# Decoder layer on one core: 512 weight columns where tokens stand, the first loads in turn, other loads and splits moved in the front

## The chip, the cores and the metric

The kernel runs on one core of one Trainium2 chip. The metric is the time of one execution on the device in microseconds (us). Five engines work beside each other, each in the order of its own program: TensorE (PE, matmuls and transposes), VectorE (DVE), ScalarE (ACT), GpSimd (POOL) and SyncE (SP, which only issues DMAs here). They wait for each other by semaphores.

## The reference

256 tokens of 1024 features pass one decoder layer in float32: a token mixer, cross attention into 256 memory tokens, and a top-4-of-32 mixture of experts, each followed by a layer norm with a residual.

```
proj = x @ w_in      # 1024 x 3600: ml q,k,v,o, gates i,f, gd q,k,v,z, gates b,a
h_ml = rms_norm(mlstm_chunkwise(q, k, v, i_pre, f_pre)) * sigmoid(ml_o)
qkv  = silu(causal_depthwise_conv([gd_q, gd_k, gd_v], gd_conv))
h_gd = rms_norm(gated_delta_chunkwise(l2(q), l2(k), v, g, beta)) * silu(gd_z)
x    = layer_norm(alpha * x + concat(h_ml, h_gd) @ w_out)
x    = layer_norm(alpha * x + softmax((x wq)(mem wk)^T / 16) (mem wv) @ wo)
x    = layer_norm(alpha * x + sum over the 4 best experts of gate * swiglu(x w_gu) w_down)
```

The weights of the first two parts have some 31 MB, those of the experts 403 MB.

## The kernel before

The program has a front (mixer and cross attention) and the expert stage behind it. In the front the weights come through a ring of six buffers of 1 MB, most as 1024 rows x 256 columns, loaded on SP's queue in the order of use (class Block, L193). `split` (L216) cuts a half of a block (128 x 1024 elements on the chip) into two fp32r parts that sum to it: the upper part is a copy on ACT (L225), the lower a subtraction (L226) on DVE, or on POOL for the second halves of the blocks named in `pool_split` (L235). The parts lie in three buffers named `whl`. `products` (L237) then makes three matmuls for each pair of tiles: upper by upper (L275), lower by upper and upper by lower (L277, L278). In some products features stand (weights are the stationary operand and 256 tokens stream); in others tokens stand and 256 weight columns stream: mv, mo, gz (parts of w_in), wout, wv and wxo.

ORDER (L36) gives the order of the w_in blocks: gk, gv, gq, gz are key, value, query and gate z of the gated delta heads, mk, mv, mq, mo those of the mLSTM heads. Between the products run "lanes" (class Lanes, L54): generators that issue a few instructions, tell for how long the engine PE is kept busy and after how long they want to go on, and wait for names that others put into a set. The lanes that matter here:

- `gates` (L397): the product of x with the gate columns (ps_g), tanh on ACT (r_f, r_i, RA; L415 to L417), softplus by exp and ln (r_e, r_t), scans on DVE (cum L434, RD L438). Then PE transposes RA and RD (ps_c, L449, L450).
- `post_k` (L490): convolution and silu of the keys (kT, L488, on DVE), then the transposes of the keys on PE (ps_t, L500), once the gates are done. `post_v` has the same for the values (vy, L488; ps_t, L521).
- `gdn_prepare` (L560) forms the matrices of the delta rule (ps_gb, ps_kk, dl, du, ps_nt), `solve` (L655) solves them, `mlstm_pair` has sd from ps_cm (L838 to L845).
- `post_res` (L929) adds the residual (L933) and takes the statistics (L934) of the layer norm.

gk0's load and x's (transposed) load are in quarters, x first. The broadcast loads of four norm vectors are issued on ACT's queue at the start.

Of the kernel before, what the change touches and what calls it, by code (L numbers as in the profile page):

```python
# [35 lines left out]
ORDER = "gk0 mv0 gk1 mk0 mq0 gq0 gv0 mo0 mv1 gv1 gz0 gq1 mo1 gz1"  # L36
# [74 lines left out]
def kernel(  # L111
# [62 lines left out]
    xt_in = chunk("xt_in").rearrange("p (k t) -> p k t", k=KT)  # L174
    for q in range(4):
        nc.sync.dma_start(xt_in[:, 2 * q:2 * q + 2, :], x_t[q * 256:q * 256 + 256, :].rearrange("(k p) t -> p k t", p=P))
# [13 lines left out]
    gph, gpl = (wt([P, 2, KT, 4, 32], "whl", F32R, n, bufs=3)[:, 0] for n in ("gph", "gpl"))  # L190
# [4 lines left out]
    class Block:  # L195


        def __init__(self, src, c0, name, then=None, rows=None):
            self.src, self.c0, self.name, self.then, self.rows = src, c0, name, then, rows

        def load(self):
            if self.rows is not None:
# [3 lines left out]
                self.parts = [None, None]  # L206
                return
            self.tv = chunk(self.name).rearrange("p (k c) -> p k c", k=KT)
            for ks in [slice(k, k + 2) for k in (0, 2, 4, 6)] if self.name == "gk0" else (slice(0, KT),):
                nc.sync.dma_start(self.tv[:, ks, :],  # L210
                                  self.src[0, ks.start * P:ks.stop * P, self.c0:self.c0 + 256].rearrange("(k p) c -> p k c", p=P))
            if self.then is not None:
                self.then()
            self.parts = [None, None]

        def split(self, hf):  # L216

            if self.parts[hf] is not None:
                return
            both = wt([P, 2, 4, 256], "whl", F32R, bufs=3)  # L220
            hi, lo = both[:, 0], both[:, 1]
            eng = nc.gpsimd if self.name in pool_split and hf == 1 else nc.vector
            for ks in (slice(0, 2), slice(2, 4)) if self.name == "gk0" else (slice(0, 4),):
                src = self.tv[:, hf * 4:hf * 4 + 4][:, ks] if self.rows is None else self.tv[:, :, hf * 256:hf * 256 + 256]
                i = nc.scalar.activation(hi[:, ks], src, AF.Copy)  # L225
                j = eng.tensor_sub(lo[:, ks], src, hi[:, ks])  # L226
                if self.name == "gk0":
                    pin(i)
                    pin(j)
            self.parts[hf] = (hi, lo)  # L230
            done.add((self.name, hf))

    pool_split = ("gk1", "mk0", "gv0", "mq0", "gv1", "gq0", "gq1", "wk0", "wk1")

    def products(pieces):  # L235


        blocks = []
        for p in pieces:
            if p["blk"] not in blocks:  # L240
                blocks.append(p["blk"])
        loaded, cut, banks = [0], [0], {}

        def ahead(i):
            n = blocks.index(pieces[min(i, len(pieces) - 1)]["blk"])
# [3 lines left out]
            while cut[0] < len(pieces) and cut[0] <= i + (2 if i else 1):  # L249
                pieces[cut[0]]["blk"].split(pieces[cut[0]]["part"])  # L250
                cut[0] += 1

        for n, p in enumerate(pieces):
            blk, hf, fresh = p["blk"], p["hf"], False
            if p["ready"] is not None and not p["ready"]():
                ahead(n - 1)
                yield p["ready"]
            ahead(n)
# [5 lines left out]
            for j in p["js"]:  # L264
                o = ps[:, j * T:j * T + T]
                js = slice(j * P, j * P + P)
                for k4 in range(4):
                    k = hf * 4 + k4
                    kx = k if blk.rows is None else k4
                    if p["feat"]:  # L270
                        a = (wh[:, k4, js], wl[:, k4, js], xh[:, kx, :], xl[:, kx, :])
                    else:
                        a = (xh[:, kx, js], xl[:, kx, js], wh[:, k4, :], wl[:, k4, :])

                    nc.tensor.matmul(o, a[0], a[2], start=fresh, stop=False, skip_group_check=True)  # L275
                    fresh = False
                    nc.tensor.matmul(o, a[0], a[3], start=False, stop=False, skip_group_check=True)  # L277
                    nc.tensor.matmul(o, a[1], a[2], start=False, stop=(k == KT - 1), skip_group_check=True)  # L278
                    if p["fine"]:
                        yield 0.32  # L280
                if not p["fine"]:
                    yield 1.28
            for lane in p["after"]:
                lanes.add(lane(ps), 0.3)
# [104 lines left out]
    for q in range(4):  # L389
# [3 lines left out]
        if q == 0:  # L393
            pin(nc.scalar.activation(gph[:, :, :, 0:4], gst, AF.Copy))
            pin(nc.vector.tensor_sub(gpl[:, :, :, 0:4], gst, gph[:, :, :, 0:4]))

    def gates():  # L397
# [9 lines left out]
        yield 2.6, 0.3  # L407
# [82 lines left out]
    def post_k(hp):  # L490
        def lane(ps):
# [5 lines left out]
            yield from wait("gates")  # L497
# [63 lines left out]
    def gdn_prepare():  # L561
# [55 lines left out]
        for c in range(2):  # L617
            lanes.add(solve(c), 1.5 * c)
        rsqrt(rk, ssq, rkt)
# [1121 lines left out]
```

## Time and profile before

| | us |
|---|---|
| median of 3 runs | 1254.56 |
| lowest, highest | 1253.55, 1255.59 |
| the profiled execution | 1253.94 |
| its span in the profile | 1252.3 |
| first expert matmul in it | 304.35 |

In that execution PE has work for 1162.0 us (93% of the span), DVE for 395.4, ACT for 242.4 and POOL for 76.7. In the second part of the page the span stands in 40 slices of 31.3 us. The first ten are the front: there DVE is busy at 5 to 8 tenths, and the DMA engines at 2 to 9. In the others PE and DMA stand at 9, and the DMA engines move 416 to 418 GB/s.

### The profile page before, as it was taken

How to read it: one execution, taken by the hardware profiler on the slowest of the kernel's cores; microseconds unless marked ns; L12 is line 12 of the kernel's file. 1: busy time of each engine (PE TensorE's matmuls, PEld its weight loads, DVE VectorE, ACT ScalarE, POOL GpSimd, SP SyncE). 2: the span in 40 equal slices, each digit the busy share in tenths (PEclk: the TensorE clock that was granted, in tenths of full speed). 3: DMA queues.
4: the chain of work that ended last, by engine and by line, in shares of the span. 5: the costliest groups of instructions: out<-in, count | busy, mean ns of one | idle time of the engine just before them, and what ended most of it. 6: DMA issues, size and time to landing. Idle time of an engine off the chain costs nothing. (4 is left out here: it accounts for less than half of the span.)

```text
span 1252.3 us, 15908 instructions
## 1 busy us (share of the span) xinstructions
PE 1162.0 (93%) x6521; PEld 618.0 (49%) x6521; DVE 395.4 (32%) x967; ACT 242.4 (19%) x448; POOL 76.7 (6%) x91
## 2 busy tenths in 40 slices
PE   7899999999999999999999999989999799999895
PEld 7889899997434343443434332323233334323244
DVE  7786888565211111121111111111121112111124
ACT  5445544452101110101111010101010001100011
POOL 5241130003000000000000000000000000000001
PEclk9899999999999999999999999999999899999998
DMA  9523268787999999999999999999999999999996
GB/s 326 184 75 102 69 209 313 269 322 282 395 374 418 416 417 417 417 418 417 417 418 417 416 417 417 416 417 417 417 416 417 417 405 418 416 417 418 417 353 167
DMA packets 125176, 446.67 MB, mean 357 GB/s; under 512 B 8550, under 2 KB 57958, under 8 KB 92330
## 3 DMA queue, kind: packets, MB, share of 16 engines
q1 hardware_dynamic: 124092, 443.63, 89.8%
q10 hardware_dynamic: 1008, 1.99, 0.4%
q8 instruction: 53, 0.87, 0.3%
q14 instruction: 23, 0.19, 0.0%
HBM read 444.54 MB, written 1.05 MB: 356 GB/s over the span
## 5 line engine op out<-in xcount | busy, mean ns | idle before, releaser
L107 PE MATMUL ps_glu<-gu,xe 128*64 128x512 f32 x1024 | 268.5, 603 | 22.5 <-DMA gu<-in_exp_w_gu_dram 16.1
L107 PE MATMUL ps_lin<-gu,xe 128*64 128x512 f32 x1024 | 264.2, 594 | 0.0
L107 PE MATMUL ps_y<-dn,ay 128*64 128x512 f32 (+1 forms) x1216 | 233.5, 530 | 19.8 <-DMA dn<-in_exp_w_down_dram 12.1
L1461 DVE TENSOR_SCALAR glu<-ps_glu 128x512 f32<-128x512 f32 x30 | 20.8, 692 | 534.6 <-PE ps_glu L107 534.6
L107 PEld LDWEIGHTS ps_y<-dn,ay 128*64 128x64 f32 x1216 | 78.7, 136 | 157.1 <-issue 113.0
L107 PEld LDWEIGHTS ps_glu<-gu,xe 128*64 128x64 f32 x1024 | 67.7, 137 | 175.3 <-issue 115.5
L107 PEld LDWEIGHTS ps_lin<-gu,xe 128*64 128x64 f32 x1024 | 74.1, 138 | 147.4 <-issue 147.1
L1462 ACT ACTIVATE glu<-glu 128x512 f32<-128x512 f32 x30 | 18.9, 630 | 514.8 <-DVE glu L1461 514.8
L1496 DVE COPY ay<-ps_y 64x512 f32<-64x512 f32 x29 | 20.0, 689 | 170.2 <-PE ps_y L107 170.2
L107 PE MATMUL acc<-ay,gp 128*128 128x512 f32 (+1 forms) x152 | 61.6, 547 | 3.7 <-DVE ay L1496 2.9
L107 POOL TENSOR_TENSOR o<-o,gb 128x512 f32<-128x512 f32 x3 | 4.2, 1409 | 936.6 <-DVE rs L107 934.4
L107 PE MATMUL ps_x<-oh,x 128*128 128x128 f32 x512 | 60.3, 275 | 1.3 <-DVE oh L1282 1.1
L107 PEld LDWEIGHTS ps_x<-oh,x 128*128 128x128 f32 x512 | 59.6, 192 | 3.6 <-DVE oh L1282 1.3
L1473 ACT ACTIVATE ay<-ps_at 128x512 f32<-128x512 f32 x30 | 17.9, 597 | 115.8 <-PE ps_at L107 115.8
L107 PEld LDWEIGHTS acc<-ay,gp 128*128 128x128 f32 x152 | 24.3, 189 | 32.2 <-issue 15.0
L1425 DVE TENSOR_SCALAR ohg<-iom,rank,Gh 128x64 f32<-128x64 f32 x120 | 33.2, 309 | 11.9 <-PE ps_x L107 11.9
L1441 ACT ACTIVATE bs<-ident 128x256 fp32r<-128x256 f32 x30 | 12.2, 411 | 99.7 <-PE ps_gp L107 94.1
L107 PE MATMUL ps_at<-ident,glu 128*128 128x128 f32 x128 | 20.9, 286 | 11.2 <-DVE gp L1429 11.2
L107 PEld LDWEIGHTS ps_at<-ident,glu 128*128 128x128 f32 x128 | 13.5, 140 | 27.8 <-DVE gp L1429 14.8
L1351 ACT ACTIVATE xe<-ps_x 128x512 f32<-128x512 f32 x32 | 19.1, 597 | 36.0 <-PE ps_x L107 36.0
L1465 DVE SCALAR_TENSOR_TENSOR glu<-glu 128x512 f32<-128x512 f32 x30 | 20.6, 688 | 0.0
L1464 DVE SCALAR_TENSOR_TENSOR glu<-glu 128x512 f32<-128x512 f32 x30 | 20.6, 685 | 0.0
(505 smaller groups left out, 1688.1 us busy)
## 6 DMA issues: line engine op xcount, KB each, us to landing
gu<-in_exp_w_gu_dram SPq DMA_DIRECT2D x256, 1024.0 KB, 19.9
dn<-in_exp_w_down_dram SPq DMA_DIRECT2D x120, 1024.0 KB, 20.0
dn<-in_exp_w_down_dram SPq DMA_DIRECT2D x14, 512.0 KB, 7.4
wout<-in_w_out_dram SPq DMA_DIRECT2D x4, 1024.0 KB, 4.9
wk<-in_xa_wk_dram SPq DMA_DIRECT2D x4, 1024.0 KB, 7.1
wv<-in_xa_wv_dram SPq DMA_DIRECT2D x4, 1024.0 KB, 6.4
wq<-in_xa_wq_dram SPq DMA_DIRECT2D x4, 1024.0 KB, 5.0
wxo<-in_xa_wo_dram SPq DMA_DIRECT2D x4, 1024.0 KB, 5.0
```

Of the source, the lines that this page charges most:

```text
L107: return lambda *a, **k: self.tc.keep_in_program_order(f(*a, **k))
L1351: nc.scalar.activation(xe_of(b)[:, q * 4:q * 4 + 4, :], ps.rearrange("p (k s) -> p k s", k=4), AF.Copy)
L1425: nc.vector.tensor_scalar(og_[:, c, j], iom, rk[c][j], gh[c][j], ALU.is_equal, ALU.mult)
L1441: nc.scalar.activation(bs.rearrange("p (q s) -> p q s", q=4), sel.unsqueeze(2).to_broadcast([P, 4, 64]), AF.Copy)
L1461: nc.vector.tensor_scalar(gl, pgu[0], 7.0, None, ALU.min)
L1462: nc.scalar.activation(th, gl, AF.Tanh, scale=0.851)
L1464: nc.vector.scalar_tensor_tensor(li, li, 1.0, gl, ALU.add, ALU.mult)
L1465: nc.vector.scalar_tensor_tensor(li, th, 1.0, li, ALU.add, ALU.mult)
L1473: nc.scalar.activation(act[1][:, b], pv, AF.Copy)
L1496: nc.vector.tensor_copy(act[2][rows_of(b, 0), 0, :], py[rows_of(b, 0), :])
```

## The change

1. **512 columns.** The weights of mv, mo, gz, wout, wv and wxo are loaded as 512 rows x 512 columns, and one matmul streams 512 columns where two streamed 256. A split now covers 256 rows x 512 columns, and the work that follows such a product goes by halves of the tokens.
2. **Start.** The quarters of x and gk0 are loaded in turn, gk0's products stand between the products of the gates, and gk0's parts have two of the three `whl` buffers, the gates' weights the third.
3. **Loads.** The four broadcast loads go from ACT's queue at the start to SP's queue behind gq0.
4. **Splits.** gv0, gv1, gq1 leave `pool_split`, and the lower part of mem (L1024) goes from POOL to DVE.
5. **Keys.** Their transposes wait for `rk` (the end of gdn_prepare) in place of `gates`. The first two solve lanes get a delay of 3.0 before the rsqrt.
6. **Order.** "gk0 mv gk1 mk0 mq0 gq0 gv0 mo gv1 gq1 gz", and the second mLSTM pair waits for the first.

```diff
-ORDER = "gk0 mv0 gk1 mk0 mq0 gq0 gv0 mo0 mv1 gv1 gz0 gq1 mo1 gz1"
+ORDER = "gk0 mv gk1 mk0 mq0 gq0 gv0 mo gv1 gq1 gz"
...
     for q in range(4):
-        nc.sync.dma_start(xt_in[:, 2 * q:2 * q + 2, :], x_t[q * 256:q * 256 + 256, :].rearrange("(k p) t -> p k t", p=P))
+        qs, rows = slice(2 * q, 2 * q + 2), slice(q * 256, q * 256 + 256)
+        nc.sync.dma_start(xt_in[:, qs, :], x_t[rows, :].rearrange("(k p) t -> p k t", p=P))
+        nc.sync.dma_start(gk0_in[:, qs, :], w_in[0, rows, C_GK:C_GK + 256].rearrange("(k p) c -> p k c", p=P))
...
-    gph, gpl = (wt([P, 2, KT, 4, 32], "whl", F32R, n, bufs=3)[:, 0] for n in ("gph", "gpl"))
+    gphl = wt([P, 2, KT, 4, 32], "whl", F32R, "gphl", bufs=3)
+    gph, gpl = gphl[:, 0], gphl[:, 1]
+    gk0_parts = [wt([P, 2, 4, 256], "whl", F32R, "gk0hl", bufs=3) for _ in range(2)]
...
+            n, w = (4, 256) if self.rows is None else (2, 512)
+            both = wt([P, 2, n, w], "whl", F32R, bufs=3)
             hi, lo = both[:, 0], both[:, 1]
...
+            src = self.tv[:, i * n:i * n + n]
+            nc.scalar.activation(hi, src, AF.Copy)
+            (nc.gpsimd if self.name in pool_split and i == 1 else nc.vector).tensor_sub(lo, src, hi)
...
-    pool_split = ("gk1", "mk0", "gv0", "mq0", "gv1", "gq0", "gq1", "wk0", "wk1")
+    pool_split = ("gk1", "mk0", "mq0", "gq0", "wk0", "wk1")
...
+                if c is None:
+                    o = ps[:, j * T:j * T + T]
+                    a = (wh[:, k_, js], wl[:, k_, js], xh[:, kx, :], xl[:, kx, :])
+                else:
+                    o = ps
+                    a = (xh[:, kx, js], xl[:, kx, js], wh[:, k_, :], wl[:, k_, :])
...
-        yield 2.6, 0.3
+            if k % 2:
+                yield 0.7, (1.4 if k < KT - 1 else 0.3)
...
-            yield from wait("gates")
+            yield from wait("rk")
             pt = psum("ps_t")
...
+        yield 0.0, 3.0
         rsqrt(rk, ssq, rkt)
...
-        yield from wait("gates", "mq", "mk", f"mv{hp}")
+        yield from wait("gates", "mq", "mk", "mv0", "mv1", *((("ml0", 0), ("ml0", 1)) if hp else ()))
...
+    def loads_between():
+        nc.sync.dma_start(mnw, mlstm_norm_w.to_broadcast([P, 512]))
+        nc.sync.dma_start(gnw, gdn_norm_w.to_broadcast([P, P]))
+        nc.sync.dma_start(x2d, x[0].rearrange("(c p) f -> p c f", p=P))
+        for src, tag in ((ln1_g, "lng"), (ln1_b, "lnb")):
+            norm_1.append(ct([P, D], tag))
+            nc.sync.dma_start(norm_1[-1], src.to_broadcast([P, D]))
...
+    def post_res(jp, st, c):
         def lane(ps):
...
+            for j in (2 * jp, 2 * jp + 1):
+                js = slice(j * 256, j * 256 + 256)
+                nc.vector.scalar_tensor_tensor(x_sb[c][:, js], x_sb[c][:, js], ALPHA, ps[:, j % 2 * 256:j % 2 * 256 + 256],
+                                               ALU.mult, ALU.add)
+                nc.vector.bn_stats(st[:, c, j, :], x_sb[c][:, js])
...
-        nc.gpsimd.tensor_sub(mts[1][:, qs, :], mem_sb[:, qs, :], mts[0][:, qs, :])
+        nc.vector.tensor_sub(mts[1][:, qs, :], mem_sb[:, qs, :], mts[0][:, qs, :])
```

Where the instructions stand changes at three places on which the prediction rests. The first is ACT's row at the start of the program, around the gates' tanh (r_f, r_i, RA). Before:

```order
L716 DMA mnw<-in_mlstm_norm_w_dram 128x512
L926 DMA lng<-in_ln_g_dram 128x1024
L926 DMA lnb<-in_ln_b_dram 128x1024
L400 ACTIVATE sgn<-sml 32x1
L225 ACTIVATE whl<-gk_244 128x512 x4
L415 ACTIVATE r_f<-ps_g,b_138 32x256
L416 ACTIVATE r_i<-ps_g,b_138 32x256
L417 ACTIVATE RA<-ps_g 32x256
L225 ACTIVATE whl<-mv_249 128x1024 x2
L424 ACTIVATE r_e<-r_t 64x256
```

After the change:

```order
L406 ACTIVATE gk0hl<-gk_in 128x512
L400 ACTIVATE xth<-xt_in 128x512
L406 ACTIVATE gk0hl<-gk_in 128x512
L412 ACTIVATE sgn<-sml 32x1
L228 ACTIVATE whl<-mv_234 128x1024 x2
L428 ACTIVATE r_f<-ps_g,b_144 32x256
L429 ACTIVATE r_i<-ps_g,b_144 32x256
L430 ACTIVATE RA<-ps_g 32x256
L228 ACTIVATE whl<-mv_236 128x1024
L496 ACTIVATE cv_y<-pp_gk_242,sml 128x256
L437 ACTIVATE r_e<-r_t 64x256
```

The two copies for mv's parts now stand ahead of r_f, a third one and a convolution step ahead of r_e, and the broadcast loads are gone from here.

The second place is PE's row around the transposes of the gates, ps_c. Before, where mv's last product of 256 columns and gk1's first one stand around them:

```order
L275 MATMUL pp_mv_346<-whl,xth 128x256
L277 MATMUL pp_mv_346<-whl,xth 128x256
L278 MATMUL pp_mv_346<-whl,xtl 128x256
L449 MATMUL ps_c<-ident,RA 128x64
L450 MATMUL ps_c<-ident,RD 128x64
L568 MATMUL ps_gb<-RD,ident 128x128 x7
L275 MATMUL pp_gk_435<-xth,whl 128x256
```

After, where mv's product of 512 columns stands before and behind (the rows from the first mv product on number 18 ahead of ps_c):

```order
L282 MATMUL pp_mv_336<-whl,xth 128x512
L284 MATMUL pp_mv_336<-whl,xth 128x512
L285 MATMUL pp_mv_336<-whl,xtl 128x512
L462 MATMUL ps_c<-ident,RA 128x64
L463 MATMUL ps_c<-ident,RD 128x64
L582 MATMUL ps_gb<-RD,ident 128x128
L282 MATMUL pp_mv_373<-whl,xth 128x512
```

The transposes ps_c stand behind 18 products of 512 columns of mv, where before they stood behind 48 of 256; before ps_c there is thus less work.

The third place is PE's row at the transposes of the keys, ps_t with kT. Before, the first of the four stands between the products of gk1:

```order
L277 MATMUL pp_gk_435<-xtl,whl 128x256
L278 MATMUL pp_gk_435<-xth,whl 128x256
L500 MATMUL ps_t<-ident,kT_171 128x128
L275 MATMUL pp_gk_435<-xth,whl 128x256
L277 MATMUL pp_gk_435<-xtl,whl 128x256
```

After, all four stand behind the first mLSTM scores, ps_st:

```order
L285 MATMUL pp_gq_719<-xth,whl 128x256
L860 MATMUL ps_st<-mqT,mkT 128x256
L846 MATMUL ps_cm<-RD,ident 128x256
L860 MATMUL ps_st<-mqT,mkT 128x256
L860 MATMUL ps_st<-mqT,mkT 128x128 x2
L513 MATMUL ps_t<-ident,kT_185 128x128
L513 MATMUL ps_t<-ident,kT_186 128x128
L513 MATMUL ps_t<-ident,kT_187 128x128
L513 MATMUL ps_t<-ident,kT_188 128x128
```

They moved by some 180 rows. POOL's row loses three subtractions of 128 x 1024 (gv, gv, gq) and the two for mem, which stand on DVE's row now.

## Rows read from the trace of the kernel before

**Rows 1.** The page, part 2: GB/s in 40 slices of 31.3 us.

```profile
GB/s 326 184 75 102 69 209 313 269 322 282 395 374 418 416 417 417 417 418 417 417 418 417 416 417 417 416 417 417 417 416 417 417 405 418 416 417 418 417 353 167
```

**Rows 2.** Stretches: us, busy PE, PEld, DVE, ACT, POOL, granted clock, DMA share, GB/s.

```profile
28.17:38.41 10.24, 10.24 (x47) 9.43 (x47) 5.55 (x14) 3.21 (x8) 0.00 (x0) 0.50 1.08 363
69.13:72.54 3.41, 3.41 (x16) 2.79 (x17) 2.21 (x10) 0.91 (x2) 1.25 (x2) 0.50 0.74 260
...
305.00:310.00 5.00, 5.00 (x26) 1.59 (x24) 0.00 (x0) 0.87 (x3) 1.81 (x2) 1.00 0.47 172
```

**Rows 3.** What PE waited for to 305 us: us in all, times, longest.

```profile
PE ps_c L449 <- DVE RA L437: 2.6, 1, 2.6
PE ps_cm L838 <- DVE sd L845: 2.4, 1, 2.4
PE ps_t L500 <- DVE kT L488: 2.2, 2, 1.1
...
PE ps_t L521 <- DVE vy L488: 1.8, 2, 1.2
PE ps_nt L613 <- DVE dl L606: 1.7, 1, 1.7
```

**Rows 4.** Timeline of PE, ACT, DVE at the start: start us, us, engine, line.

```profile
7.67 0.29 PE L405 MATMUL ps_g<-xth,gpl 128*128 128x256 f32 x1
9.45 0.28 PE L405 MATMUL ps_g<-xth,gpl 128*128 128x256 f32 x1
...
11.49 0.45 ACT L415 ACTIVATE r_f<-ps_g,b 32x256 f32<-32x256 f32 x1
16.31 2.00 ACT L225 ACTIVATE whl<-mv 128x1024 fp32r<-128x1024 f32 x2 [3.49 <-DMA mv<-in_w_in_dram]
...
19.68 0.28 DVE L425 TENSOR_SCALAR r_w<-r_e 64x256 f32<-64x256 f32 x1
26.42 0.41 DVE L437 SCALAR_TENSOR_TENSOR RA<-r_i,cum 32x256 f32<-32x256 f32 x1
```

**Rows 5.** Timeline of POOL and DVE, where both work on large tiles.

```profile
122.91 2.35 POOL L107 TENSOR_TENSOR whl<-gq,whl 128x1024 fp32r<-128x1024 f32 x1 [13.80 <-ACT whl L225]
...
53.07 0.42 DVE L488 SCALAR_TENSOR_TENSOR kT<-cv_s,cv_y 128x256 f32<-128x256 f32 x1
123.16 2.37 DVE L488 SCALAR_TENSOR_TENSOR vy<-cv_s,cv_y 128x256 f32<-128x256 f32 x1 [1.22 <-ACT cv_s L487]
170.91 3.46 DVE L226 TENSOR_TENSOR whl<-wout,whl 128x1024 fp32r<-128x1024 f32 x1 [1.36 <-ACT whl L225]
```

**Rows 6.** DVE's subtractions for wv: ns min/median/max, first and last start.

```profile
L226 DVE TENSOR_TENSOR whl<-wv,whl x8: 1219/1226/1227, 202.3 to 223.3; 128x1024 fp32r<-128x1024 f32 x8
```

**Rows 7.** Stretches with products of mo, wout, wv, wxo alone; first busy time: PE.

```profile
136.72:142.26 5.54, 5.54 (x48) 5.51 (x48) 0.00 (x0) 1.00 0.01 3
167.42:180.92 13.50, 13.50 (x116) 13.46 (x114) 1.50 (x4) 1.00 1.03 312
208.41:230.17 21.76, 21.76 (x192) 21.72 (x192) 2.05 (x3) 1.75 (x3) 1.00 0.87 319
272.19:280.82 8.63, 8.63 (x72) 8.58 (x72) 0.52 (x2) 1.00 0.97 391
```

**Rows 8.** Timeline of PE in the expert stage: products of 512 columns.

```profile
1032.60 0.40 PE L107 MATMUL ps_glu<-bgl,bs 128*128 128x512 f32 x1
1032.83 0.40 PE L107 MATMUL ps_lin<-bgh,bs 128*128 128x512 f32 x1
...
305.26 1.03 PE L107 MATMUL ps_lin<-gu,xe 128*64 128x512 f32 x4
306.11 1.03 PE L107 MATMUL ps_glu<-gu,xe 128*64 128x512 f32 x4
```

**Rows 9.** Timeline of DVE behind the last wxo product.

```profile
293.80 0.41 DVE L933 SCALAR_TENSOR_TENSOR x<-x,pp_wxo 128x256 f32<-128x256 f32 x1
294.24 0.43 DVE L934 BATCH_NORM_STATS2 st<-x 128x6 f32<-128x256 f32 x1
```

More of the change, by code (lines that the diff above doesn't have):

```diff
@@ L199, in __init__ @@
             self.src, self.c0, self.name, self.then, self.rows = src, c0, name, then, rows
+            self.parts = [(t[:, 0], t[:, 1]) for t in gk0_parts] if name == "gk0" else [None, None]
         def load(self):
+            if self.name == "gk0":
+                return
             if self.rows is not None:
@@ L738, in gdn_states @@
     def gdn_states():
-        yield from wait("um0", "v0", "v1")
+        yield from wait("um0", "v0", "v1", "kt0", "kt1")
         vn0 = bv[0]
@@ L897, with piece @@
     jobs = []
[L899 to L903 removed]
+    def piece(blk, part, key, k0, xs_, c=None, kx=0, after=None, ready=None, bank=pp, fine=False):
+        jobs.append(dict(blk=blk, part=part, key=key, k0=k0, xs=xs_, c=c, kx=kx, after=after, ready=ready, bank=bank, fine=fine))
@@ L904, in job, with wide @@
+    def job(src, c0, name, xs_, post, ready=None, then=None, bank=pp):
         blk = Block(src, c0, name, then)
-        piece(blk, 0, xs_, feat, ready=ready, bank=bank)
-        piece(blk, 1, xs_, feat, (post,))
-    xs_of_x = lambda: xs
+        for i in range(2):
+            piece(blk, i, blk, 4 * i, xs_, after=post if i else None, ready=None if i else ready, bank=bank)
+    def wide(blk, xs_, c, part, after=None, **kw):
+        last = blk.rows == 1 and part == 1
+        piece(blk, part, (id(blk.src), blk.c0, c), blk.rows * 4 + part * 2, xs_, c, after=after if last else None, **kw)
@@ new lines, in wide_job @@
+    def wide_job(src, c0, name, xs_, post, then=None, bank=pp):
+        for r in range(2):
+            blk = Block(src, c0, f"{name}{r}", then if r else None, rows=r)
+            order = [(c, i) for c in range(2) for i in range(2)]
+            for c, part in order if bank is pp and r == 0 else [(c, i) for i, c in order]:
+                wide(blk, xs_, c, part, post(c), bank=bank)
+    norm_1 = []
+    def loads_between():
[5 more added lines that the diff above has]
+            nc.sync.dma_start(norm_1[-1], src.to_broadcast([P, D]))
@@ L955, in layer_norm @@
         done.add((flag, c))
-    g1 = bcast(ln1_g, "lng")
-    b1 = bcast(ln1_b, "lnb")
     st1 = ct([P, 2, 4, 6], "ln_st")
-    wouts = [Block(w_out, j * 256, f"wout{j}") for j in range(4)]
+    wouts = [[Block(w_out, jp * 512, f"wout{hf}{jp}", rows=hf) for jp in range(2)] for hf in range(2)]
     for hf in range(2):
-        for j in range(4):
-            flag = ("mixed", 1) if hf else "gdn_banks" if j == 2 else ("mixed", 0)
-            piece(wouts[j], hf, lambda: ms, False, (post_res(j, st1),) if hf else (),
-                  (lambda f: lambda: f in done)(flag), pp if j < 2 else sv)
-    lanes.add(layer_norm(0, st1, g1, b1, "x1"))
-    lanes.add(layer_norm(1, st1, g1, b1, "x1"))
+        for jp in range(2):
+            flag = ("mixed", 1) if hf else "gdn_banks" if jp else ("mixed", 0)
+            for part in range(2):
+                for c in range(2):
+                    wide(wouts[hf][jp], lambda: ms, c, part, post_res(jp, st1, c), ready=(lambda f: lambda: f in done)(flag),
+                         bank=sv if jp else pp)
+    lanes.add(layer_norm(0, st1, norm_1, "x1"))
+    lanes.add(layer_norm(1, st1, norm_1, "x1"))
     lanes.run(products(jobs))
@@ L1093, in lane @@
             yield 0.0, 1.4
-            yield from wait(f"vm{h}")
+            yield from wait(f"vm{h}0", f"vm{h}1")
             po = sv("ps_o")
```

215 lines of the change are left out of this document (98 added, 117 removed).

## Prediction, written before the changed kernel ran

> **What bounds the kernel now.** I read the page's slices first. From the thirteenth slice on, the DMA engines move 416 to 418 GB/s in nearly every one [rows 1]: the expert stage lasts as long as its weights take to arrive, and the change leaves that stage alone. In the first ten slices the rate is 69 to 326 GB/s, so the front is not a matter of bandwidth. Is the end fixed by the front, then? At 305 to 310 us, when the first expert's products run, the DMA engines stand at a share of 0.47 and 172 GB/s [rows 2]: the buffers for expert weights are full and loads wait for PE to free one. A front that ends X earlier frees them X earlier, so X in the front is X at the end. I price the change in the front alone, up to the first expert matmul at 304.35 us.
>
> In the front PE is nearly always at work, so two things count: the waits of PE, and the length of one product. The waits come from one view [rows 3]: 2.6 us for RA (the gates), 2.4 for sd, 2.2 for kT, 1.8 for vy, 1.7 for dl, each for DVE. Then there are two stretches at half the granted clock (0.50, the level of 1.2 GHz): 10.24 and 3.41 us [rows 2]. The first begins 1.3 us behind the end of the wait for RA (26.8, below), the second shortly behind that for sd. At half clock the work of 10.24 us is worth 5.1, that of 3.41 worth 1.7.
>
> **The start (costs 2.8).** Before, the last gate product begins at 9.45 [rows 4], r_f at 11.49, and RA is written at 26.42 + 0.41 = 26.83. After the change, 36 of gk0's 48 products stand ahead of the last gate product, which is number 60 of 72. PE steps by 0.118 us there (15 steps from 7.67 to 9.45 [rows 4]), so the 36 products put the last one at 9.45 + 36 x 0.118 = 13.7, through at 14.0. Loads don't hold it up: r_f stood behind gk0's four copies on ACT and began at 11.49, so both loads were there by then. Next, the two copies for mv stand ahead of r_f on ACT, and the first takes the buffer that held the gates' weights, so it can't begin before 14.0. Two copies last 2.00 [rows 4]: r_f begins at 16.1, 4.6 later than before. The copies had cost something before as well: they came at 16.31, after 3.49 us of waiting for mv's load, and r_e stood behind them, so r_w began only at 19.68. From there to RA's end it took 26.83 - 19.68 = 7.15, with one subtraction of 1.22 among it. After the change r_f, r_i and RA's tanh take 1.3 (to 17.4), DVE has the two mv subtractions until 17.5, four steps of 0.41 like RA's, and a third subtraction of 1.22 [rows 6] ahead of r_w, which begins near 20.4. From r_w on 7.15 - 1.22 remain, and four or five steps of the convolution of 0.4 us each come in between: RA's end near 28.3, 1.4 later. Ahead of it PE has done 24 + 48 + 18 x 2 = 108 units of 256 columns, before 24 + 48 + 48 = 120: another 12 x 0.116 = 1.4 of work is left over. Together 2.8 later. Bounds: 0 (if the scheduler's insertions fall into gaps) and 5.6 (r_f's delay of 4.6 passes through and only 1.0 of the 1.4 remains on top).
>
> The wait of PE ahead of ps_c grows from 2.6 to some 6 us (mv's 18 products end near 21). I take the half-clock stretch behind it as before, 10.24 us; bounds: shorter by 3 us of work gained, or a second one of the same length, 5.1.
>
> The broadcast loads that leave the start free the way for mv's load, which is what ACT waited for (3.49); that gain is already in the chain above, where the copies no longer wait for DMA. On SP's queue they now stand ahead of gv0's load; before gv0 is needed there is a slack of tens of us at 69 to 102 GB/s in the third to fifth slice [rows 1], so I cost them at nothing; without that cover they would cost their bytes, 1.3 MB at the 363 GB/s of [rows 2], 3.6.
>
> **Keys (gains 2.2).** The two waits for kT go: the transposes now stand behind ps_st, long after kT is written. The work that fills the place is gk1's and mk's products, which are ready. Who waits instead is gdn_states, for the scaled keys, and it comes tens of us later. Bounds: 0 and 2.5. The wait for dl (1.7) stays: its chain, ssq to br to dl, is the same.
>
> **sd (gains 1.0, and half of 1.7).** sd stands behind a row of DVE steps; gv0's subtraction moves to DVE (+1.22), but the POOL subtraction beside it goes. With the solve lanes delayed by 3.0, sd comes earlier among them. I take 1.4 of the 2.4 as left, and a chance of one half that the short half-clock stretch behind it goes with it: 1.0 + 0.85. Bounds: -1.2 (the added subtraction, nothing gained) and 4.1.
>
> **Less splitting on POOL (gains 1.9).** What a POOL subtraction of 128 x 1024 does to DVE shows in the profile [rows 5]: vy, 0.42 long where POOL rests (the kT row at 53.07 has the same shape), takes 2.37 while POOL works from 122.91 for 2.35. PE waits 1.2 for that vy, 1.8 over both. gv1 and gq1 leave POOL, and the block of 1.95 goes; I take 1.9. DVE gets five subtractions of 1.22 [rows 6], 6.1 in all, and loses about as much in blocked time: 1.95 at vy, 3.46 - 1.22 = 2.24 at wout's subtraction beside mem's [rows 5], and the like beside gv0. Hence nothing for mem and for the stretch from 160 to 200. Bounds for this part: -1.2 and 2.5.
>
> **512 columns (gains 4.1).** Half of the front's products change: mv, mo and gz 144, wout, wv and wxo 96 each, 432 matmuls for 864. What 256 columns cost stands in dense stretches [rows 7]: mo 5.54 / 48 = 115.4 ns, wout 13.50 / 114 = 118.4, wv 21.76 / 192 = 113.3, wxo 8.63 / 72 = 119.9. The 864 take 288 x 115.4 + 192 x (118.4 + 113.3 + 119.9) = 100.7 us. For 512 columns two rows bound it [rows 8]. A single-pass product of the same shape and type in the expert stage begins 0.23 us after the one before (1032.60 to 1032.83): 432 x 231 ns = 99.8, a gain of 0.9. In a dense run with 64 weight columns four take 0.855 (305.26 to 306.11), 214 each: 92.4, a gain of 8.3. The former stands among products of other shapes, the latter has narrower weights. Nearest to what will run are the dense rows of 256 themselves: over half of 214 they carry (100.7 - 92.4) / 864 = 9.6 ns each. Paid once per matmul instead of twice that leaves 432 x 9.6 = 4.1.
>
> The Trainium skill ("TensorE: Matmul & The Clock Gate", section "Wait — 56ns, not 53.3ns?") has a rule against a surcharge of that size: a warm matmul starts N / 2.4 GHz plus about 2.5 ns after the last one, 215.7 ns for 512 columns. By it 256 columns would take 109 and the exchange would save 432 x 2.5 = 1.1; the rows of 256 show 113 to 120, so something more than the rule is paid there, and whether 512 columns pay it too is open.
>
> **The tail (costs 0.7).** Behind the last wxo product stood one residual step (0.41) and one statistics step (0.43) [rows 9]; now there are two of each for the last 512 columns. One pair more, 0.7 to 0.84 with the overlap of their starts; nothing covers it, since the layer norm and the routing hang on it.
>
> **Sum.** 2.8 - 2.2 - 1.85 - 1.9 - 4.1 + 0.7 = -6.55. On the profiled execution's 1253.94 that is 1247.4; the median of the runs, 1254.56, lies 0.6 above it, and by it 1248.0, which I predict.
>
> **Rivals.**
> *512 columns at 214 ns.* Then the change gains 8.3 there, 4.2 more: 1243.8. For it: the rate is there in this profile, seven such groups of four in a row, of which the rows show two starts. Against: their weights are half as wide.
> *No change.* The gate chain is 4 later instead of 2.8, sd's wait and its half-clock stretch stay, 512 columns gain 0.9: 4 - 2.2 - 1.9 - 0.9 + 0.7 = -0.3, 1254.3. For it: PE's waits are waits for DVE, and DVE is given 6.1 us more.
> *Slower, by the gates.* r_f's 4.6 pass through to RA and gk1's start: +5.6. The wait ahead of ps_c, then 9 us, is followed by two half-clock stretches of 10.24 in place of one, +5.1. sd hangs on the gates, so its gain goes. 5.6 + 5.1 - 2.2 - 1.9 - 4.1 + 0.7 = +3.2; with the 512 columns' lower bound, +6.4; between them 1259. It decides from RA's end at about 31 on. For it: the clock fell after each of the two long waits. Against: DVE's steps before RA have gaps that the delay can use.
>
> **Chances.** Forecast 0.50 (its own range 1244.5 to 1251.5), 512 columns at 214 ns 0.17, no change 0.19, slower 0.14. What counts as no change is 0.2%, 2.5 us, so faster is below 1252.1 and slower above 1257.1. Faster takes nearly all of the first two: 0.66. Within 0.2%: 0.18 from the third and a little of the first. Slower: 0.16. The range goes to 1240 below, where the second case meets the upper bounds of keys and sd, and to 1257.5 above, which leaves out most of the last case.
>
> **What would show it.** RA's subtraction should end near 28.3, no wait for kT stand in PE's list, vy's step last 0.42 with no POOL work beside it, 512-column products follow each other by 214 to 231 ns (near 222), and the first expert matmul begin near 298, with the expert stage as long as before. I am wrong if RA's end lies past 31, if a second stretch at 0.50 stands in the first 70 us, or if wout, wv and wxo wait for DVE's split parts.

## The result and the profile after

| us | before | after |
|---|---|---|
| median of 4 runs each | 1254.05 | 1241.42 |
| lowest, highest | 1252.40, 1255.59 | 1240.55, 1242.17 |
| the profiled execution | 1253.94 | 1242.05 |
| its span | 1252.3 | 1240.1 |
| first expert matmul in it | 304.35 | 291.78 |

The ratio of the times is 0.9889 with a 95% interval of 0.9874 to 0.9903: 12.2 to 15.8 us faster, twice the 6.55 of the sum. 1241.42 lies in the range but outside the forecast's own (1244.5 to 1251.5). The first expert matmul begins 12.57 us earlier, the span is 12.2 shorter: the premise held that a us in the front is a us at the end. From that matmul to the end it is 947 to 950 us in the traces of all runs here (951.4 in one), so two fronts can be compared directly, too. The page's slices show the expert stage at the same rate as before [rows 1]:

```profile
GB/s 333 189 103 103 75 308 268 230 378 315 378 385 417 416 416 417 417 416 417 416 417 417 417 417 417 417 417 417 417 417 416 417 403 418 417 417 417 418 354 162
```

To see what kind of time went, I added up PE's steps (from the start of one instruction to that of the next) from 5.3 us to the first expert matmul, in three sorts. A step counts as a wait from 370 ns on (in a half-clock stretch from 600).

| us | before | after | difference |
|---|---|---|---|
| waits | 26.0 | 16.85 | -9.15 |
| steps in half-clock stretches | 13.5 | 8.56 | -4.94 |
| all other steps | 259.5 | 261.05 | +1.55 |

So the time came from waits and from the clock. The other steps, where 864 matmuls became 432, did not shrink; with the half-clock steps counted at half their length, the work is 266.3 us before and 265.3 after. The list of what PE waited for, to 295 us of the changed kernel (us in all, times, longest), shows which waits are left:

```profile
PE ps_c L462 <- DVE RA L450: 4.8, 1, 4.8
PE pp_mv L284 <- DVE whl L229: 2.4, 2, 1.6
...
PE ps_kk L606 <- DVE kT L501: 0.7, 1, 0.7
...
PE pp_mq L282 <- DVE cv_y L498: 0.4, 1, 0.4
PE ps_cm L846 <- DVE sd L853: 0.2, 1, 0.2
```

Against [rows 3], RA's wait grew from 2.6 to 4.8; those for sd (2.4), kT of ps_t (2.2), vy (1.8) and dl (1.7) are gone or down to 0.2. (In the second trace of the changed kernel 0.7 is left for sd and 0.2 for wk.) The waits for mv's lower parts are 2.4, where 0.9 stood before and 0.7 for the upper ones. One more is gone that the prediction had passed over, though it stood fourth in the same list of the kernel before:

```profile
PE pp_wk L278 <- DVE whl L226: 2.0, 2, 1.7
```

All six waits of the kernel before that are named here have something in common. Ahead of each stands a DVE step beside a POOL subtraction, and the step ends with that subtraction, whatever its own length, or one own length behind it. For vy it is in [rows 5]; for RA and sd it follows below; wk's step takes 2.88 beside POOL's for the other half of wk, where 1.22 is usual. For kT and for br, on which dl hangs, it reads:

```profile
38.89 2.41 POOL L107 TENSOR_TENSOR whl<-mk,whl 128x1024 fp32r<-128x1024 f32 x1 [12.76 <-ACT whl L225]
39.15 2.43 DVE L488 SCALAR_TENSOR_TENSOR kT<-cv_s,cv_y 128x256 f32<-128x256 f32 x1 [1.50 <-ACT cv_s L487]
...
56.32 2.39 POOL L107 TENSOR_TENSOR whl<-gq,whl 128x1024 fp32r<-128x1024 f32 x1 [6.87 <-ACT whl L225]
56.40 2.41 DVE L602 TENSOR_TENSOR br<-rk,gcols 128x4 f32<-128x4 f32 x2
```

The second kT that PE waits for, at 47.38, takes 2.35; alone kT takes 0.42 [rows 5]. The two steps of br take 0.24 in the changed kernel, where POOL's subtraction for gq begins behind them.

The stretches at half clock of the changed kernel (us, busy PE, PEld, DVE, ACT, POOL, granted clock, DMA share, GB/s), to be read beside [rows 2]:

```profile
21.87:32.11 10.24, 5.59 (x14) 4.25 (x15) 6.75 (x20) 2.66 (x5) 0.00 (x0) 0.50 1.07 377
...
288.11:291.52 3.41, 3.25 (x15) 3.25 (x16) 1.14 (x7) 0.60 (x1) 0.00 (x0) 0.50 0.43 123
```

The first is as long as before, but PE has work in only 5.59 of its 10.24 us, since it begins inside the wait for RA; before, PE worked through all 10.24. The one behind sd is gone, and a new one of 3.41 lies on the routing matmuls right before the first expert.

The timeline of PE, ACT and DVE at the start (start us, us, engine, line), beside [rows 4]:

```profile
12.74 0.28 PE L417 MATMUL ps_g<-xth,gphl 128*128 128x256 f32 x1
...
12.89 2.01 ACT L228 ACTIVATE whl<-mv 128x1024 fp32r<-128x1024 f32 x2 [1.94 <-DMA mv<-in_w_in_dram]
14.80 0.45 ACT L428 ACTIVATE r_f<-ps_g,b 32x256 f32<-32x256 f32 x1
...
19.83 0.69 DVE L438 TENSOR_SCALAR r_w<-r_e 64x256 f32<-64x256 f32 x1
...
23.46 0.73 DVE L447 TENSOR_TENSOR_SCAN cum<-ones_r,r_t 64x128 f32<-64x128 f32 x2
...
25.70 0.40 DVE L450 SCALAR_TENSOR_TENSOR RA<-r_i,cum 32x256 f32<-32x256 f32 x1
```

r_f is 3.3 later than before (4.6 forecast), r_w 0.15 later, and RA is written at 26.10, 0.73 earlier than before where 1.4 later was forecast. Between r_w and RA lie the two scans: 0.73 us here. In the kernel before, the same two took 2.89, beside POOL's subtraction for gk1:

```profile
22.82 2.89 DVE L434 TENSOR_TENSOR_SCAN cum<-ones_r,r_t 64x128 f32<-64x128 f32 x2
...
22.90 2.54 POOL L107 TENSOR_TENSOR whl<-gk,whl 128x1024 fp32r<-128x1024 f32 x1 [5.83 <-DVE whl L226]
```

After the change POOL does that subtraction 12 us later, when the gates are through:

```profile
35.35 2.40 POOL L107 TENSOR_TENSOR whl<-gk,whl 128x1024 fp32r<-128x1024 f32 x1 [14.97 <-ACT whl L228]
```

vy's steps, 2.37 beside POOL before [rows 5], all take 0.42 now (ns min/median/max, first and last start):

```profile
L501 DVE SCALAR_TENSOR_TENSOR vy<-cv_s,cv_y x4: 418/418/421, 93.8 to 122.9; 128x256 f32<-128x256 f32 x4
```

### The profile page after: what moved, and what is told of

The parts are those of the page before. It is cut to its first block, busy times and chain, and to the rows that moved or that the text cites. A ratio compares the mean times of both kernels' runs of the same rounds, so it can differ in the third digit from the quotient of the medians.

```text
span 1240.1 us, 15027 instructions
## 1 busy us (share of the span) xinstructions
PE 1156.8 (93%) x6087; PEld 593.1 (48%) x6087; DVE 384.4 (31%) x968; ACT 242.9 (20%) x444; POOL 72.8 (6%) x85
## 5 line engine op out<-in xcount | busy, mean ns | idle before, releaser
L1472 ACT ACTIVATE bs<-ident 128x256 fp32r<-128x256 f32 x30 | 12.2, 410 | 99.9 <-PE ps_gp L107 94.2
L107 PEld LDWEIGHTS ps_at<-ident,glu 128*128 128x128 f32 x128 | 13.5, 140 | 27.8 <-DVE gp L1460 14.8
```

Source lines behind the costliest of these rows:

```text
L107: return lambda *a, **k: self.tc.keep_in_program_order(f(*a, **k))
L1472: nc.scalar.activation(bs.rearrange("p (q s) -> p q s", q=4), sel.unsqueeze(2).to_broadcast([P, 4, 64]), AF.Copy)
```

## The experiments

All but the last group undo or do one thing. Each number is a median with the ratio to runs of the kernel before on the same chip and its 95% interval. "Against the changed kernel" sets the ratio against 0.9889 (for gv0, mem and the second run of the bank against 0.9897, the changed kernel's beside them), times 1254; such a difference of two ratios is uncertain by 2 to 3 us, so the 2.6, 1.6 and 2.5 below are hardly clear of nothing by themselves.

**The changed kernel once more.** Unchanged, with the third group of runs.

> The changed kernel once more, beside the others of this group: 1240 to 1243, ratio 0.989.

1242.09, ratio 0.9897 (0.9879 to 0.9915): the result stands.

**512 columns undone.** Each product of 512 columns as two of 256; loads, splits and order stay.

```diff
-                nc.tensor.matmul(o, a[0], a[2], ...)
+                for hs in (slice(0, 256), slice(256, 512)) if c is not None else (slice(0, T),):
+                    nc.tensor.matmul(o[:, hs], a[0], a[2][:, hs], ...)
```

> The changed kernel with every product of 512 columns done as two of 256 (same stationary operand, same weights in the same buffers); all else as changed. The prediction's step (a fixed surcharge of some 10 ns per matmul, paid once instead of twice) expects 4.1 us more than the changed kernel, near 1245.5. The rival from the trace of the changed kernel (512 columns begin 233 to 236 ns after each other, so a pair of 256 at 115 to 118 costs the same) expects no difference: within 1 us of 1241.4, and steps of 113 to 120 ns in wout, wv and wxo.

1243.13, 0.9910 (0.9897 to 0.9924): 2.6 more than the changed kernel. Two stretches with wv's products and two with wxo's alone show the steps, first of the changed kernel, then of this one (the first busy time is PE's):

```profile
194.74:217.14 22.40, 22.40 (x96) 17.86 (x96) 1.73 (x3) 1.78 (x3) 1.00 0.67 234
...
261.05:269.49 8.44, 8.44 (x37) 6.76 (x37) 0.52 (x2) 1.00 0.92 369
```

```profile
196.00:218.61 22.61, 22.61 (x192) 22.57 (x192) 1.76 (x3) 1.77 (x3) 1.00 0.63 216
...
262.91:271.56 8.65, 8.65 (x72) 8.59 (x72) 0.47 (x2) 1.00 0.94 366
```

One matmul of 512 takes 233 ns in wv (22.40 / 96) and 228 in wxo (8.44 / 37); a pair of 256 takes 235.5 and 240. The difference per pair is 2 to 12 ns, not the 9.6 taken throughout. Against the kernel before it is less: there a pair of 256 took 226.7 in wv and 239.7 in wxo [rows 7], so 512 columns are 6.6 ns slower in wv and 11.6 faster in wxo. Taken over all six products, the mean step from start to start (at full clock and without waits) times their number gives 104.3 us for the 864 of the kernel before, 104.3 for the 432 of the changed kernel and 107.0 for the 864 of this run. The other traces with the 864 of the kernel before have 104.3 to 105.6, those with the 432 have 103.7 to 104.3. So the 2.6 is what the undoing costs; by these steps the change itself gained nothing between the two profiled executions, and at most 1.9. The Trainium skill ("TensorE: Matmul & The Clock Gate", section "Wait — 56ns, not 53.3ns?") has 215.7 ns for 512 columns; neither stretch comes to it.

**The splits undone, and done alone.** First, in the changed kernel, gv0, gv1, gq1 and mem go back to POOL. Its edit, whose reverse in the kernel before is the second run:

```diff
-    pool_split = ("gk1", "mk0", "mq0", "gq0", "wk0", "wk1")
+    pool_split = ("gk1", "mk0", "gv0", "mq0", "gv1", "gq0", "gq1", "wk0", "wk1")
...
-        nc.vector.tensor_sub(mts[1][:, qs, :], ...)
+        nc.gpsimd.tensor_sub(mts[1][:, qs, :], ...)
```

> The changed kernel with the second halves of gv0, gv1, gq1 and the lower part of mem back on POOL. The prediction's step (only the wait for vy comes back) expects 1.9 us more than changed, 1243.3. The rival (each large POOL subtraction stops a DVE step of a chain that PE waits for: sd, vy, and wk behind mem) expects 4 to 6 us more, 1245.5 to 1247.5, with waits of PE for sd, vy and wk's split part back in its list.

1246.41, 0.9933 (0.9919 to 0.9948): 5.5 more, where the sum had 1.9. Its waits (the profiled execution, 1251.3, was its longest, so I read only waits from it):

```profile
PE ps_cm L846 <- DVE sd L853: 2.4, 1, 2.4
PE pp_wk L285 <- DVE whl L229: 1.7, 1, 1.7
```

The waits for sd and wk are back, that for vy, on which the forecast's 1.9 rested, is not.

> The kernel before with one part of the change alone: gv0, gv1, gq1 and mem's lower part subtracted on DVE. The prediction's step (only vy's wait goes) expects 1.9 us less than before. The rival (every large POOL subtraction beside a DVE chain costs; undone in the changed kernel it cost some 5 us) expects 4 to 6 us less, with the waits for sd, vy and wk's part shortened in PE's list.

1245.56, 0.9941 (0.9927 to 0.9956): alone, the splits bring 7.4. In that trace the waits for vy and wk and the stretch at half clock behind sd are gone, and sd's wait is 1.1.

**gv0 alone, mem alone.** In the changed kernel, gv0 goes back to POOL:

```diff
-    pool_split = ("gk1", "mk0", "mq0", "gq0", "wk0", "wk1")
+    pool_split = ("gk1", "mk0", "gv0", "mq0", "gq0", "wk0", "wk1")
```

> The changed kernel with gv0's second half alone back on POOL. Theory: that one subtraction stands beside the chain rk, sd and costs most of what the four together cost (5.5): 3 to 4.5 us more than changed, the wait for sd of 2.4 back and a half-clock stretch behind it. The prediction's step had put the cost at vy, which this kernel leaves on DVE: by it nothing or 1 us less (one subtraction of 1.22 fewer on DVE).

1245.61, 0.9933 (0.9916 to 0.9951): 4.5 in one subtraction (3.5 by the medians of this group of runs). The timeline of POOL and DVE around it:

```profile
65.48 2.38 POOL L107 TENSOR_TENSOR whl<-gv,whl 128x1024 fp32r<-128x1024 f32 x1 [3.53 <-issue]
65.57 2.37 DVE L636 TENSOR_TENSOR rk<-rk,gcols 128x4 f32<-128x4 f32 x2
67.87 0.34 DVE L851 SCALAR_TENSOR_TENSOR sd<-ps_cm,gcols,up_neg 128x128 f32<-128x128 f32 x1
```

The stretch behind it (columns as above):

```profile
69.17:76.00 6.83, 6.83 (x32) 5.80 (x30) 4.97 (x10) 3.91 (x10) 2.18 (x4) 0.50 0.43 151
```

In the changed kernel the same two steps of DVE, each of four elements a partition, take:

```profile
69.19 0.23 DVE L636 TENSOR_TENSOR rk<-rk,gcols 128x4 f32<-128x4 f32 x2
```

A tiny step takes ten times as long and ends with POOL's subtraction. sd stands right behind it in DVE's row, PE waits 1.7 for sd, and a stretch of 6.83 us at half clock follows, full of work (3.4 us at full clock). 1.7 + 3.4 = 5.1. The profiled execution, the fastest of its six, does not show all of it in the front: the first expert matmul begins at 294.20, 1.8 to 2.4 behind the changed kernel's two (291.78, 292.36), for RA's wait is 0.8 shorter in it and the half-clock stretch near 290 us is missing. So the mechanism is shown, its price only as 2 to 5 us. In the kernel before the same can be read:

```profile
64.64 2.38 POOL L107 TENSOR_TENSOR whl<-gv,whl 128x1024 fp32r<-128x1024 f32 x1
...
65.10 1.96 DVE L315 SCALAR_TENSOR_TENSOR rk<-rkt,rk 128x8 f32<-128x8 f32 x1
66.98 0.34 DVE L843 SCALAR_TENSOR_TENSOR sd<-ps_cm,gcols,up_neg 128x128 f32<-128x128 f32 x1
```

mem alone goes back with the second part of the same edit:

> The changed kernel with mem's lower part alone back on POOL. Theory: 1.5 to 2.5 us more than changed, as PE's wait for wk's part of 1.7. The prediction's step (nothing either way between 160 and 200 us): within 1.

1244.20, 0.9917 (0.9902 to 0.9931): 2.5. wk's wait is back, as long as with all four undone (1.7). DVE's subtraction for wout beside mem's takes 2.22 instead of 1.22, and with that DVE comes to wk later: POOL's own subtraction for wk now begins first (168.87 against 169.40), and DVE's takes 2.96.

**Keys undone, and done alone.** In the changed kernel the transposes wait for the gates again; in the kernel before they wait for rk (there gdn_states also waits for the scaled keys).

```diff
-            yield from wait("rk")
+            yield from wait("gates")
             pt = psum("ps_t")
```

> The changed kernel with the keys' transposes waiting for the gates again. Theory of the prediction: the two waits for kT come back, 2.2 us more, 1243.6. Rival: with other loads and order kT is no longer late, and nothing comes back, 1241.4; or it comes back in full and the DVE row around it moves too, 3 or more.

1242.51, 0.9902 (0.9887 to 0.9917): 1.6. Waits for kT (1.3) and dl (1.7) are back. So is wk's (2.1), though mem stays on DVE here: POOL's subtraction for wk begins at 169.47, DVE's at 169.83, and DVE's takes 3.15. Against that the steps at half clock in the front are 4.25 us in this trace, 8.56 in the changed kernel's. So the 1.6 is not the price of kT's waits alone.

> The kernel before with the keys' transposes alone moved behind rk. The prediction's step expects 2.2 us less than before, the two waits for kT gone. Rival: the wait moves on to the next step that needs DVE (ps_kk, ps_nt), and the gain is under 1.

1252.11, 0.9982 (0.9970 to 0.9994): 2.3 alone, as the sum had it. PE's list tells more: the two waits for kT are gone, but 0.7 for kT at ps_kk, 1.6 for X and 0.9 more for gk0's parts stand in their place, dl keeps 1.4, and sd's falls from 2.4 to 0.4. PE's waits are 25.1 us in all, 0.9 less than before.

**POOL off the scans, in the kernel before.** gk1's subtraction goes to DVE; nothing else.

```diff
-    pool_split = ("gk1", "mk0", "gv0", "mq0", "gv1", "gq0", "gq1", "wk0", "wk1")
+    pool_split = ("mk0", "gv0", "mq0", "gv1", "gq0", "gq1", "wk0", "wk1")
```

> The kernel before with gk1's second half subtracted on DVE in place of POOL. Theory on the start: the two scans of 2.89 us in the gates' chain were held up by POOL's subtraction for gk1 beside them; without it they last about 0.7, RA is written 2.1 us earlier, PE's wait of 2.6 for RA nearly goes, and the kernel is some 2 us faster than before. The prediction's reading (the scans last 2.89 by themselves) expects no change, or 1.2 more for the added subtraction.

1248.51, 0.9962 (0.9946 to 0.9977): 4.8 faster than the kernel before, for one word; in the trace the first expert matmul begins at 298.68, 5.7 earlier. The scans in DVE's timeline:

```profile
23.45 0.72 DVE L434 TENSOR_TENSOR_SCAN cum<-ones_r,r_t 64x128 f32<-64x128 f32 x2
```

Its first stretch at half clock:

```profile
20.23:23.64 3.41, 3.41 (x19) 3.41 (x18) 3.20 (x8) 2.23 (x4) 0.00 (x0) 0.50 1.10 348
```

The wait for RA is gone, and of 10.24 us at half clock 3.41 remain.

**The gates' products at once again.** In the changed kernel, one `yield 2.6, 0.3` behind the loop in place of the ones between.

```diff
-            if k % 2:
-                yield 0.7, (1.4 if k < KT - 1 else 0.3)
+        yield 2.6, 0.3
```

> The changed kernel with the gates' products issued at once again, nearly all of them ahead of gk0's (only 6 of gk0's stand between them). The prediction's step (interleaving puts the gates' end, and so r_f and RA, later, and the start costs 2.8) expects RA earlier and 1.4 to 2.8 us less than the changed kernel, 1239.3 to 1240.7. Rival: x and gk0 arrive in turn, so PE waits for x's last quarter instead, gk0's end moves by as much, and RA comes at the same time or not more than 1 earlier: within 1 us of changed, or later.

1247.63, 0.9946 (0.9933 to 0.9958): some 6 to 7 slower than the changed kernel. The rival's "or later" covers the time but not the way to it: RA comes 3.2 earlier and its wait falls from 4.8 to 0.9. In DVE's timeline:

```profile
22.46 0.41 DVE L449 SCALAR_TENSOR_TENSOR RA<-r_i,cum 32x256 f32<-32x256 f32 x1
```

Its stretch at half clock:

```profile
23.79:37.44 13.65, 11.47 (x38) 9.44 (x39) 8.52 (x26) 5.07 (x11) 0.00 (x0) 0.50 0.91 324
```

And in the list of PE's waits:

```profile
PE ps_kk L605 <- DVE kT L500: 2.5, 2, 1.6
...
PE ps_nt L626 <- DVE dl L619: 1.4, 1, 1.4
...
PE ps_c L461 <- DVE RA L449: 0.9, 1, 0.9
```

The half-clock stretch is 13.65 us long with 11.47 of work in it, and kT and dl are late: the later kT takes 2.31 and the steps of br 2.47 beside POOL's subtractions for mq and gq. So an early RA by itself does not make the end early. The edit moved more rows than the gates' (ps_kk stands ahead of mv's second product here), so it does not price the interleaving by itself.

**What PE lacks during the wait for RA.** Two edits of the changed kernel. One fixes mv's products, ps_c and the first ps_gb in the order of the program:

```diff
+                keep = pin if blk.name in ("mv0", "mv1") else (lambda i: i)
-                nc.tensor.matmul(o, a[0], a[2], ...)
+                keep(nc.tensor.matmul(o, a[0], a[2], ...))
...
-        yield 0.0, 4.5
+        yield 0.0, 3.4
```

> The changed kernel with PE's row at the gates held in the order of the program: 36 products of mv ahead of the transposes ps_c instead of 18 (and the first ps_gb behind them). Theory: the 4.8 us in which PE waits for RA are filled with the 18 products that now run behind it at half clock, and the clock does not fall: mv's end comes some 5 us earlier, 1236.5. Rival: the gates' chain then sets the rest of the front, and what is gained at mv is waited for behind it (mv's fourth part, gk1's parts): 1239 to 1241.

1242.73, 0.9904 (0.9891 to 0.9918): no gain. PE now stands before mv's product of the second half of the tokens:

```profile
PE pp_mv L283 <- DVE cmi L454: 10.1, 1, 10.1
```

The list names cmi, which ends at 28.13. That product's PSUM bank is the one that gk0's product holds until the convolution has read it, and the convolution's last read ends at 28.06, between the steps of the gates' chain; PE goes on at 28.21. The other edit gives it another bank:

```diff
-                wide(blk, xs_, c, part, post(c), bank=bank)
+                wide(blk, xs_, c, part, post(c), bank=sv if name == "mv" and c == 1 else bank)
```

> The changed kernel with one edit: mv's product for the second half of the tokens gets another PSUM bank (of the four 'sv' banks) in place of the one that gk0's product holds until its convolution is read. In the run with PE's row held in program order, PE waited 10 us at just that product, so theory says: the wait of 4.8 for RA in the changed kernel is a lack of work, not the gates' lateness; with a bank free the scheduler puts 46 mv products of 512 columns ahead of ps_c, PE stays busy, the clock does not fall, and the front ends 4 to 7 us earlier: 1235 to 1237. Rival: the gates' chain sets the pace of what follows (gdn_prepare) and gives the time back: 1240 to 1241.

1238.23, 0.9878 (0.9863 to 0.9893). The same kernel again, beside the changed kernel:

> The changed kernel with the other PSUM bank for mv's second half of the tokens, once more beside the changed kernel. Theory (PE's idle time at the gates was a lack of work): 2 to 5 us less than the changed kernel. Rival (the gates' chain gives it back): within 1.

1239.24, 0.9879 (0.9860 to 0.9898), where the changed kernel has 0.9897 (0.9879 to 0.9915): 1.4 and 2.3 us by the ratios, within their uncertainty. The traces are clearer: the first expert matmul begins at 287.32 and 287.98, 3.8 to 5.0 earlier than in the changed kernel's two. PE's wait for RA falls from 4.8 to 2.4, the wait for kT at ps_kk grows from 0.7 to 1.8. What stays of it can be read around 27 us:

```profile
26.56 2.38 POOL L107 TENSOR_TENSOR whl<-gk,whl 128x1024 fp32r<-128x1024 f32 x1 [5.62 <-DVE kT L501]
...
26.97 2.12 DVE L448 COPY RD<-cum 32x256 f32<-32x256 f32 x1
```

With the bank free, gk1's subtraction comes earlier on POOL and lies on the gates' chain again.

**Both together.** The bank, and gk1's subtraction on DVE (`pool_split = ("mk0", "mq0", "gq0", "wk0", "wk1")`); then the bank and no split on POOL at all (`pool_split = ()`).

> The changed kernel with the other PSUM bank for mv and gk1's second half subtracted on DVE. In the run with the bank alone a copy in the gates' chain (RD, 32 x 256) took 2.12 us beside POOL's subtraction for gk1. Theory: without it RA comes 1.8 us earlier, PE's wait of 2.4 for RA nearly goes, 1.5 to 2.5 us less than with the bank alone: near 1237. Rival: the added 1.22 on DVE stands ahead of gk1's products and takes it back: 1239.

1232.92, 0.9827 (0.9815 to 0.9840).

> The changed kernel with the other PSUM bank for mv and no weight subtraction on POOL at all: gk1, mk0, mq0, gq0, wk0, wk1 too go to DVE. Theory (a large subtraction on POOL costs DVE about what it saves, and hits whatever chain stands beside it): the same as with gk1 alone on DVE or 1 to 2 less, 1235 to 1237. Rival (DVE is full from 38 to 69 us, 27.95 of 31 busy before the change, and six subtractions of 1.22 more make it the bound): 2 to 4 more, 1239 to 1241.

1231.92, 0.9824 (0.9809 to 0.9839). Both beat both kernels: some 22 us below the one before, some 8 below the changed one, and they do not differ by more than their intervals. gk1 on DVE without the bank was not tried in the changed kernel, so the two parts of this gain are not told apart. In the first of them RD's copy reads:

```profile
26.42 0.28 DVE L448 COPY RD<-cum 32x256 f32<-32x256 f32 x1
```

and the stretch from 11 to 280 us, at a granted clock of 1.00:

```profile
11.00:280.00 269.00, 262.57 (x1757) 232.84 (x1756) 212.34 (x535) 141.88 (x258) 52.22 (x60) 1.00 0.65 230
```

No half-clock stretch is left there; one of 3.41 on the routing matmuls, behind 280 us, stays. PE's wait for RA is 0.6 in both.

## Why the prediction was right in sign and wrong in size

- **Splits: the step that failed first.** "Less splitting on POOL (gains 1.9)" was priced at vy alone, "hence nothing for mem and for the stretch from 160 to 200". Undone, the splits cost 5.5; done alone they bring 7.4. The row for vy [rows 5] was read rightly as DVE held by POOL, but the same was not looked for at the other steps that PE waits for. It stands there at every one: rk's step of 1.96 right ahead of sd, kT's of 2.43 and 2.35, br's of 2.41 ahead of dl, and wk's wait of 2.0. In the two traces the waits for sd, kT, vy, dl and wk lost 9.9 us, where the sum had 5.1 for them (1.0, 2.2, 1.9, nothing and nothing). gv0 alone is worth 4.5, mem 2.5 (7.0 together against 5.5, within the uncertainty).
- **sd** was forecast at 1.0 and half of 1.7, with a lower bound of a loss, as a matter of DVE's queue length. Of the 2.4 all but 0.2 (0.7 in the second trace) went, and the whole stretch of 3.41; the bound of 4.1 named there is nearly what came. That rk is no longer held is one cause: gv0 back on POOL brings 1.7 of the wait back, and the splits alone took it to 1.1. It is not the only one: with the keys alone it falls to 0.4, though rk's step still takes 2.29 there. What the delay of the solve lanes adds was not tried.
- **The start: the second step that failed.** "Costs 2.8" rested on "from r_w on 7.15 - 1.22 remain". Those 7.15 us held the scans' 2.89, of which 2.2 was POOL's subtraction for gk1, which the change moves out of the way. The steps ahead of r_w were forecast too late by 0.6. RA's wait came out at 4.8 (some 6 forecast), and the half-clock stretch, "taken as before", has half its time over idle PE: its loss is 2.8 (half of 5.59) instead of 5.1. That the whole start is about even (some 2 more in waits, some 2.4 less in the clock) is worked out from the two traces. The run in the kernel before with gk1's subtraction on DVE shows the mechanism: 4.8.
- **Keys: right in size, the account not shown.** 2.2 forecast; 2.3 alone, 1.6 undone. But neither trace shows just the two waits going and coming: alone, most of what they leave is taken by others, and undone, wk's wait comes along. What made kT late, POOL's subtractions for mk and mq, was not seen.
- **dl: wrong, small.** Its 1.7 did not stay; 0.7 for kT at ps_kk and 0.4 for cv_y came in its place. "Its chain, ssq to br to dl, is the same" holds for the order of the steps; but in the kernel before br was held by POOL's subtraction for gq, and in the changed kernel it is through when that begins. Where dl's wait is in the list, a step of this chain is held: br with the keys alone (1.4; the two steps take 2.46), rkt with the keys at the gates again (1.7; rkt takes 2.37 where 0.12 is usual). With gk1 on DVE, where br is through when POOL begins, the wait is gone.
- **512 columns: the third step that failed.** 4.1 forecast (0.9 to 8.3). Undone it costs 2.6, but in the kernel before and in the changed one the steps of these products sum to the same 104.3 us (nothing to 1.9 over all traces). The forecast took 9.6 ns as paid once per matmul; one of 512 columns costs 228 to 233 ns, a pair of 256 had cost 227 to 240. The rival of 214 ns is refuted by the same two numbers.
- **Tail: right, with an addition.** Two residual and two statistics steps now stand behind the last product [rows 9]:

```profile
278.89 0.74 DVE L959 SCALAR_TENSOR_TENSOR x<-x,pp_wxo 128x256 f32<-128x256 f32 x2
279.55 0.74 DVE L961 BATCH_NORM_STATS2 st<-x 128x6 f32<-128x256 f32 x2
```

  From the first start to the last end they take 1.40 where 0.87 was. The half-clock stretch at 288 us costs half of its 3.25 us of work more, 1.6, which the forecast had not.
- **What would show it wrong.** Neither a second half-clock stretch before 70 us, nor RA past 31, nor products of wout, wv or wxo waiting for their parts appeared.

The parts undone one by one sum to 5.5 + 1.6 + 2.6 = 9.7 of some 13; without the 2.6, which the steps of the two kernels do not show, to 7.1. The other 3 to 6 us belong to the start, the order and the loads by subtraction only. The broadcast loads' part was not tried by itself, nor the delay of the solve lanes. Open is also why wv's 256-column step is 113.4 ns in the kernel before [rows 7] and with the splits alone, and 117.8 (22.61 / 192) in the run with 256 columns, with the keys alone and with gk1 on DVE. In the last two nothing was changed at these products.

## What to carry to other kernels

Where a helper engine does large elementwise work, look at every step on the path beside it for a duration out of line with its size, not only at the one that the list of waits names: steps of 0.2 to 0.7 us that take 2 to 3 were worth more here than the whole exchange of 864 matmuls for 432, which by the steps gave 1.9 at most. Price a half-clock stretch by the work in it, not by its length: the same 10.24 us cost 5.1 where PE was busy and 2.8 where half of it fell on a wait. When PE waits for one late tile, ask also what else it could have run and which buffer holds that back.

## What the runs showed of the hardware

- A POOL subtraction of 128 x 1024 holds DVE steps with two inputs in SBUF until its end, whatever their size: 2.3 us for 128 x 4 elements, 2.56 for a scan of 64 x 128 (0.39 in the changed kernel), 2.37 for vy. Steps of DVE that read one input from PSUM and run beside it kept their time. The Trainium skill ("SBUF — State Buffer", section "Who interferes with whom") says that such a pair shares a port for whole instructions, and that who begins first decides. The traces agree, also on the second half: in the changed kernel POOL's subtraction for wk takes 3.50 where DVE's began at the same time and took its usual 1.22. Two steps with one input were held too: RD's copy (2.12 against 0.28) and rkt of 128 x 8 in the run with the keys at the gates (2.37 against 0.12). The two for wk:

```profile
168.34 1.22 DVE L229 TENSOR_TENSOR whl<-wk,whl 128x1024 fp32r<-128x1024 f32 x1
...
168.34 3.50 POOL L107 TENSOR_TENSOR whl<-wk,whl 128x1024 fp32r<-128x1024 f32 x1 [1.15 <-ACT whl L228]
```

- The stretches at half clock change in place and length from kernel to kernel: the first one of the changed kernel, 10.24, is 6.83 us long in three of the kernels with one part undone (512 columns, splits, keys). Two executions of one kernel, the one with the other bank, have their stretch of 3.41 at 49.62 and at 31.52. So a profile's half-clock stretch is not a fixed cost of one wait.
- The stretch of 3.41 at 288 us is there in the changed kernel's other profile too, and absent in the kernel before and in three of the kernels with one part undone (512 columns, keys, gv0). What decides it stays open.
